# An encoder layer on one Trainium2 core: one directly multiplied half in the up projection instead of three, and whole h put together by DMA

## The chip, the cores and the metric

The kernel runs on one core of a Trainium2 chip. A core has a matrix engine (PE; its weight loads are listed as PEld), a vector engine (DVE), a scalar engine (ACT), a general engine (POOL) and a queue engine (SP). Each engine works through its own instructions strictly in order, and waits at the head of its queue until the semaphores of an instruction allow it to start. DMAs are issued from SP's queue and from POOL's queue, and all of them are carried out by the same 16 DMA engines. The metric is device microseconds of one execution, and lower is better.

## The reference

One layer over 512 tokens of width 2048, in float32. The part that matters here is the second half of it:

```
x = x + rms_norm(concat(a, p) @ w_o, post_mix_g)
h = rms_norm(x, pre_ffn_g)
up = causal_dwconv(h @ w_up, conv_w, conv_b)          # 2048 -> 2 * 5632, then 3 taps along the tokens
y = (gelu(up[:, :5632]) * up[:, 5632:]) @ w_down      # 5632 -> 2048
x = x + rms_norm(y, post_ffn_g)
```

`a` and `p` are the outputs of an attention and of a pooling branch; they are not touched by the change. The scale of the second norm, one number per token, is not applied to h itself: the kernel multiplies with x times gain and scales the rows of `h @ w_up` afterwards, with a tile `R` that holds the token scales along the free axis.

## The kernel before

**Number format.** A float32 operand is held as a high part `hi` (rounded by ACT, line 140) and a low part `lo` (the rest, a DVE subtraction, line 141). `split` makes both. `mm3` multiplies with three matmuls per block: hi by hi, hi by lo, lo by hi.

**The up projection.** The 11264 columns of `w_up` are cut into 22 units, each with a gate half and a value half of 256 columns (a half is two blocks of 128 channels, `j = 0, 1`). So there are 44 halves, each with 2048 rows of weights and 512 tokens. A half can be done in two ways.

- Directly, as `mm3` over 16 blocks of 128 rows and two `j`: 96 matmuls with 512 columns. This is done for the first `PLAIN = 3` halves: gate and value of unit 0 (`ups`), and the gate of unit 1 (`up(1, 0)`).
- As a Strassen-Winograd scheme of seven products (`seven`, `mm2`). The two weight blocks per half (`m`), the two halves of the 2048 rows (`kh`) and the two halves of the tokens make 2 x 2 blocks on each side. Each of the seven products costs 8 wide matmuls (512 columns, line 170) and 8 narrow ones (256 columns, line 176) per weight part: 56 wide and 56 narrow per half. This is done for the other 41 halves, `k = 0 .. 40`.

The seven products are numbered. Products 1, 2, 7 and 4 take a quarter of h as it is; 5, 3 and 6 take sums of quarters, held in `hs[5]`, `hs[3]`, `hs[6]`; product 7 takes a difference that is written over a quarter of h itself (`h_difference`). A quarter is a half of the rows (`k`) and a half of the tokens (`t`), and each of them lies in two tiles (`i = 0, 1`), four blocks of 128 rows to a tile.

**The sums of h.** `h_sums(i)` is called for `i = 0` and then `i = 1`. It first needs whole quarters, `whole(k, t)`: the quarter's `hi` plus its `lo`, made by a DVE addition (line 1298) into a tile from the ring `x` of the pool `p3`. That ring (`raw_x`) has four buffers of 128 x 1024 floats; the raw weights of the products 1 of most halves come from it too. Out of four whole quarters come, on DVE, `a22 - a21` (split into `hs[5]`), `a11 - a21` (kept in `differences` until `h_difference` splits it), `-(a22 - a21) - a11` (split into `hs[6]`), and one more (split into `hs[3]`). So `hs[5]` is ready first, `hs[3]` last, and one buffer of the ring per `i` is held until `h_difference`.

**The weights of the seven products.** The class `Factors` holds the list `order` of all (half, product) pairs. `load` fetches raw weight blocks on SP's queue into `raw4` (five buffers) or `raw_x` tiles; `add` adds another block from DRAM onto a raw tile by an accumulating DMA on POOL's queue, which is how the weight sums of the scheme are formed; `make` splits a raw tile into a pair of `w4` tiles (eight buffers, so four pairs). `get` asks for the next pair and prefetches `AHEAD` further ones. The first products in `order` are (0, 1), (0, 2), (0, 5), (1, 1), (0, 3).

**What sets the order.** PE's instructions run in the order in which the code calls them (`manual_schedule`). For ACT, DVE, POOL and SP a planner puts instructions into each queue, by the time at which it thinks they become ready and by their place in the code; `issue_after` puts an instruction behind a named one. A tile of a ring with no free buffer waits for a release.

**Around the change.** The output projection before it ends with `keep_x` and `turn_back`: the second half of the tokens (`t0 = 2`) is finished, transposed back by PE and split into the h tiles `hT`, while `gate_part` multiplies the first direct half piece by piece, for the first half of the tokens and then for the second. The loop over `q` ends with `gate_part(3, 2)`. `keep_x(2, ...)` squares x on ACT (line 910), a reduction (line 1054) and `rstd` (DVE line 217, then a power on POOL, line 218) make the token scales `rt`. `spread2` brings `rt` into `R`: four transposes on PE (line 223) and two DVE copies (lines 1264 and 1265). `gate` and `product` then apply the taps, gelu and the product for a unit, and store it. In the kernel before, the order of PE after `gate_part(3, 2)` is: the value half of unit 0; the first quarter of `up(1, 0)`; the transposes of `spread2`; the rest of `up(1, 0)`; and then the seven products of half 0 on.

**Keeping a product.** The products accumulate in PSUM banks `a`, `g` and `d`; `keep(k, i)` takes them out. After product 1 ACT copies bank `a` (512 columns, line 1412) into `za`; after product 2 DVE adds bank `d` to it (512 columns, line 1415); `keep_all` adds the two halves of `za` (256 columns, line 1434).

Of the kernel before, what the change touches and what calls it, by code (L numbers as in the profile page):

```python
# [15 lines left out]
P = 128  # L16
# [14 lines left out]
PLAIN = 3  # L31
# [14 lines left out]
def f32(ap):  # L46
    return ap.bitcast(F32)
# [34 lines left out]
def encoder_layer(ctx: ExitStack, tc: tile.TileContext, x, xT, vecs, rel, post_mix, post_ffn,  # L82
# [800 lines left out]
    with tc.tile_pool(name="p2", bufs=1, reuse_waits="tile") as p2:  # L883
# [137 lines left out]
        ups = [[bank(f"up0_{p}_{j}") for j in range(2)] for p in range(2)]  # L1021
# [14 lines left out]
        for q in range(5):  # L1036
            if q < 4:
                x2(2, (y21, y22)[q // 2], q // 2, columns(q % 2))
                for i in range(2):
                    turn_back(2, 2 * q + i, bank(f"xt{q}{i}"))  # L1040
            if not q:
                gate_part(3, 0, slice(2, 4))
            if q:
                gate_part(q - 1, 2)
                more_sums(1)
                weights.prefetch(q)
        keep_x(2, turn_back.last)
# [154 lines left out]
    with tc.tile_pool(name="p3", bufs=2, reuse_waits="tile") as p3:  # L1202
# [43 lines left out]
        def up(u, p, between=()):  # L1246
            ps = [bank(f"up{u}_{p}_{j}") for j in range(2)]
            between = list(between)
            for i in range(4):
                w = weights.get(f"w{p}{u}_{i}")  # L1250
                factors.prefetch(4 - len(weights.specs) + weights.used)
                for kb in range(4 * i, 4 * i + 4):
                    for j in range(2):
                        mm3(ps[j], part(w, j, slice(kb % 4 * P, (kb % 4 + 1) * P)), g_both(hT, kb),
                            kb == 0, kb == KD - 1)
                step = between.pop(0) if between else None
                if step:
                    step()
            return ps

# [33 lines left out]
        def h_sums(i):  # L1294
            def whole(k, t):
                v = raw_x(f"q{k}{t}").rearrange("p (a b) -> p a b", a=4)
                hi, lo = quarter(k, t, i)
                nc.vector.tensor_add(v, f32(hi), f32(lo))
# [23 lines left out]
        class Factors:  # L1322

            RAW, AHEAD = 10, 4

            def __init__(self):
                n = 2 * NU - PLAIN

                self.alone = 0, n - 1
                place_of = {1: 0, 6: 8, 2: 2, 7: 10, 5: 4, 4: 12, 3: 6}
                begin = [(0, 1), (0, 2), (0, 5), (1, 1), (0, 3)]
                end = [(n - 1, 5), (n - 2, 6), (n - 1, 3), (n - 1, 1), (n - 2, 7), (n - 1, 6), (n - 2, 4),
                       (n - 1, 7), (n - 1, 2), (n - 1, 4)]
                order = sorted((7 * k + at, k, i) for k in range(n) for i, at in place_of.items())
                self.order = begin + [(k, i) for _, k, i in order if (k, i) not in begin + end] + end
                self.raw, self.made, self.loaded, self.used = {}, [], 0, 0

            def block(self, k, m, kh):  # L1340
                return w_up[(PLAIN + k) // 2, (PLAIN + k) % 2, m, kh]

            def load(self, k, i):
                def raw(what, tile_, m, kh):
                    nc.sync.dma_start(tile_, self.block(k, m, kh))
                    self.raw[k, what] = tile_

                if i == 1 and (k, "w") not in self.raw:
                    raw("w" if k in self.alone else "x", raw4("wx") if k == self.alone[0] else raw_x("wx"), 0, 0)
                elif i == 5 and k == self.alone[0]:  # L1350
                    raw("x", raw4("wx"), 0, 0)
                    self.add(k, "x", 1, 0)
                elif i == 5 and k == self.alone[1]:
                    raw("w", raw_x("wx"), 0, 0)
                    raw("x", raw_x("wx"), 1, 0)
                elif i == 3:
                    raw("y", raw4("wy"), 1, 1)
                elif i == 2:
                    raw("z", raw4("wz"), 0, 1)

            def add(self, k, what, m, kh):
                nc.gpsimd.dma_start(self.raw[k, what], self.block(k, m, kh), accum_op=ALU.add)  # L1362

            def make(self, k, i):
                what = {1: "w" if k in self.alone else "x", 3: "y", 7: "y", 2: "z"}.get(i, "x")
                v = self.raw[k, what]
                if (k, i) == (self.alone[1], 5):
                    nc.vector.tensor_add(v, v, self.raw[k, "w"])
                hi, lo = w4("wfh"), w4("wfl")
                split(hi, lo, v)  # L1370
                if len(self.made) == 2:
                    self.third = split.last, split.rest
                if i == 1 and k not in self.alone:
                    self.add(k, "x", 1, 0)
                elif i == 5:
                    self.add(k, "x", 1, 1)
                elif i == 6:
# [367 lines left out]
```

## Time and profile before

| | |
|---|---|
| median of 3 runs | 1860.05 us (1859.49 to 1861.0) |
| the profiled execution: time | 1858.89 us |
| its span, first to last instruction | 1857.1 us |
| DVE busy over the span | 83% |
| ACT busy over the span | 58% |
| POOL busy over the span | 16% |
| bytes moved by DMA | 426.01 MB |

The span is what the profile's times are counted from; the time of the execution is 1.79 us longer than it. Start times in the timelines below are microseconds from the start of the span. A matmul's duration in a timeline covers its way through the array, and successive matmuls overlap; so the price of a matmul is read from the distance between starts, not from its duration.

### The profile page before, as it was taken

Reading aid. Unit: us, or ns where it says so; the run is one execution under the profiler, and the core shown is the slowest. Engines: PE = TensorE matmul, PEld = TensorE weight load, DVE = VectorE, ACT = ScalarE, POOL = GpSimd, SP = SyncE. Lnnn points to the kernel's source line nnn. Section 1 sums busy time; section 2 is a strip of 40 time slices with the busy share of each in tenths; the row PEclk is TensorE's granted clock in tenths of the full one; section 3 lists DMA queues with packets and bytes.
Section 4 is the critical chain, followed back from the end, with each engine's and each line's share of the span. In section 5 each row is a group of like instructions: output and inputs, shape, how many; then the busy total and the mean of one; then the engine's idle time right before and its main releaser. Section 6 shows DMA issues by size and latency. Waiting matters only on the chain.

```text
span 1857.1 us, 25452 instructions
## 1 busy us (share of the span) xinstructions
PE 1842.6 (99%) x9598; PEld 1584.3 (85%) x9598; DVE 1532.2 (83%) x1799; ACT 1084.4 (58%) x1376; POOL 302.8 (16%) x402
## 2 busy tenths in 40 slices
PE   9999999999999999999999999999999999999998
PEld 7888888888879888888888888888888888888886
DVE  6988778878588988888887888888887899899876
ACT  7654455456564666566565665666655655565553
POOL 3411001100000112212122122121121001111101
PEclk9999999999999999999999999999999999999999
DMA  8599977998987798888888988889888977777785
GB/s 319 171 319 302 322 230 233 267 264 310 326 308 202 185 220 195 205 204 200 201 200 203 207 202 195 204 206 205 199 179 288 363 224 171 193 211 178 176 230 157
DMA packets 139338, 426.01 MB, mean 229 GB/s; under 512 B 11920, under 2 KB 15376, under 8 KB 133520
## 3 DMA queue, kind: packets, MB, share of 16 engines
q0 software_dynamic: 54864, 173.56, 45.8%
q1 hardware_dynamic: 84352, 250.84, 38.8%
q8 instruction: 75, 1.23, 0.3%
q14 instruction: 47, 0.39, 0.1%
HBM read 370.35 MB, written 104.33 MB: 256 GB/s over the span
## 4 chain that ended last, share of the span: by engine, by line
PE 69%; DMA 1%; DVE 1%; issue 0%; ACT 0%; DVEq 0%; POOLq 0%; ACTq 0%
PE qa L170 16%; PE qa L176 8%; PE qg L170 8%; PE qg L176 4%; PE qd L170 4%; PE pa L162 4%; PE pa L165 4%; PE pa L164 4%; PE qd L176 2%; PE pg L162 2%; PE pg L165 2%; PE pg L164 2%; PE up L165 1%; PE up L162 1%; PE up L164 1%; PE pd L164 1%
## 5 line engine op out<-in xcount | busy, mean ns | idle before, releaser
L140 ACT ACTIVATE wfh<-wx 128x1024 fp32r<-128x1024 f32 x192 | 203.4, 1059 | 154.3 <-PE qg L170 54.4
L170 PE MATMUL qa<-gT,wfh 128*128 128x512 f32 x1152 | 288.6, 392 | 0.0
L141 DVE TENSOR_TENSOR wfl<-wx,wfh 128x1024 fp32r<-128x1024 f32 x192 | 234.6, 1222 | 61.0 <-ACT wfh L140 44.0
L170 PEld LDWEIGHTS qa<-gT,wfh 128*128 128x128 f32 x1152 | 207.2, 189 | 37.1
L1362 POOL DMA_DIRECT2D wx<-in_w_up x122 | 104.6, 858 | 502.6 <-DVE wfl L141 467.9
L140 ACT ACTIVATE wfh<-wy 128x1024 fp32r<-128x1024 f32 x96 | 101.7, 1060 | 108.5 <-PE qg L170 57.2
L170 PE MATMUL qg<-h,wfh 128*128 128x512 f32 x656 | 162.2, 389 | 0.1
L176 PE MATMUL qa<-gT,wfl 128*128 128x256 f32 x1152 | 161.4, 283 | 0.6 <-ACT zm L1422 0.6
L176 PEld LDWEIGHTS qa<-gT,wfl 128*128 128x128 f32 x1152 | 151.5, 191 | 4.9 <-ACT zm L1422 0.8
L170 PEld LDWEIGHTS qg<-h,wfh 128*128 128x128 f32 x656 | 122.9, 188 | 25.9 <-ACT zb L1418 0.5
L141 DVE TENSOR_TENSOR bl<-b,bh 128x2048 fp32r<-128x2048 f32 x56 | 127.2, 2285 | 19.1 <-ACT bh L140 11.7
L140 ACT ACTIVATE bh<-b 128x2048 fp32r<-128x2048 f32 x56 | 106.0, 1911 | 52.8 <-DVE b L1126 21.8
L141 DVE TENSOR_TENSOR wfl<-wy,wfh 128x1024 fp32r<-128x1024 f32 x96 | 117.1, 1220 | 12.6 <-ACT wfh L140 7.8
L162 PE MATMUL pa<-bh,ah 128*128 128x512 f32 x320 | 124.5, 389 | 0.0
L164 PE MATMUL pa<-bl,ah 128*128 128x512 f32 x320 | 124.5, 389 | 0.0
L165 PE MATMUL pa<-bh,al 128*128 128x512 f32 x320 | 124.5, 389 | 0.0
L141 DVE TENSOR_TENSOR wfl<-wz,wfh 128x1024 fp32r<-128x1024 f32 x48 | 58.7, 1223 | 54.2 <-PE qa L170 54.2
L176 PEld LDWEIGHTS qg<-h,wfl 128*128 128x128 f32 x656 | 89.5, 190 | 6.4
L170 PE MATMUL qd<-gT,wfh 128*128 128x512 f32 x384 | 94.9, 389 | 0.0
L176 PE MATMUL qg<-h,wfl 128*128 128x256 f32 x656 | 91.5, 282 | 0.0
L170 PEld LDWEIGHTS qd<-gT,wfh 128*128 128x128 f32 x384 | 71.9, 188 | 14.9
L170 PE MATMUL qa<-h,wfh 128*128 128x512 f32 x328 | 82.1, 392 | 0.0
(554 smaller groups left out, 4352.5 us busy)
## 6 DMA issues: line engine op xcount, KB each, us to landing
wx<-in_w_up POOLq DMA_DIRECT2D x122, 512.0 KB, 6.2
b<-in_w_down SPq DMA_DIRECT2D x32, 1024.0 KB, 7.0
wt<-in_w_o POOLq DMA_DIRECT2D x24, 1024.0 KB, 16.8
wx<-in_w_up SPq DMA_DIRECT2D x43, 512.0 KB, 5.5
wz<-in_w_up SPq DMA_DIRECT2D x41, 512.0 KB, 5.7
wy<-in_w_up SPq DMA_DIRECT2D x41, 512.0 KB, 4.7
wy<-in_w_up POOLq DMA_DIRECT2D x41, 512.0 KB, 6.7
sum<-part POOLq DMA_DIRECT2D x38, 512.0 KB, 6.4
```

What stands on the lines that cost most here:

```text
L140: rounded = nc.scalar.activation(hi, src, AF.Copy)
L141: rest = nc.vector.tensor_sub(lo, src, f32(hi))
L162: nc.tensor.matmul(ps, l[0], r[0], start=first, stop=False, skip_group_check=onto)
L164: nc.tensor.matmul(low, l[0], r[1], start=False, stop=False, skip_group_check=onto)
L165: nc.tensor.matmul(ps, l[1], r[0], start=False, stop=last, skip_group_check=onto)
L170: nc.tensor.matmul(ps, w[0][:, kb], pairs[kb][0], start=fresh and not kb, stop=last, skip_group_check=not fresh)
L176: nc.tensor.matmul(ps[:, sl], w[1][:, kb], pair[:, sl], start=False, stop=last, skip_group_check=not fresh)
L1362: nc.gpsimd.dma_start(self.raw[k, what], self.block(k, m, kh), accum_op=ALU.add)
```

## The change

`PLAIN` becomes 1: only the gate half of unit 0 is multiplied directly. The value half of unit 0 and the gate half of unit 1 become halves `k = 0` and `k = 1` of the seven-product scheme, which now has 43 halves. `Factors` moves up, in front of the loop that multiplies the direct half, and that loop prefetches the products' weights, six raw blocks at most, until `open` is set. The list begins with products 1 and 2 of the halves 0, 1 and 2, and these three halves keep the raw tiles of product 1 apart from those of product 5 (`alone`). The token scales are spread and the first gate is computed ahead of the loop over products. `whole` no longer adds on DVE: SP copies `hi` into the tile by a DMA within the core's memory, and POOL's queue adds `lo` by an accumulating DMA. `za` shrinks to 256 columns with three buffers, so product 1 and product 2 are folded when they are taken out.

```diff
-PLAIN = 3
+PLAIN = 1
...
-        ups = [[bank(f"up0_{p}_{j}") for j in range(2)] for p in range(2)]
+        class Factors:
...
+                self.alone, self.open = (0, 1, 2, n - 1), False
+                place_of = {1: 0, 6: 8, 2: 2, 7: 10, 5: 4, 4: 12, 3: 6}
+                begin = [(0, 1), (0, 2), (1, 1), (1, 2), (2, 1), (2, 2), (0, 5), (0, 3)]
...
+                if i == 1 and (k, "w") not in self.raw:
+                    raw("w" if k in self.alone else "x", raw4("wx") if k in self.alone[:3] else raw_x("wx"), 0, 0)
+                elif i == 5 and k in self.alone[:3]:
+                    raw("x", raw_x("wx") if k else raw4("wx"), 0, 0)
+                    self.add(k, "x", 1, 0)
...
+            def prefetch(self, n):
+                ahead = self.used + n + self.RAW - self.AHEAD if self.open else 6
+                while self.loaded < min(len(self.order), ahead) and n > 0:
+                    self.load(*self.order[self.loaded])
+                    self.loaded += 1
+                while len(self.made) < min(len(self.order), self.used + n):
+                    self.make(*self.order[len(self.made)])
...
+        ups = [[bank(f"up0_{j}") for j in range(2)]]
...
                 gate_part(q - 1, 2)
                 more_sums(1)
-                weights.prefetch(q)
+                factors.prefetch(q)
         keep_x(2, turn_back.last)
-        for q in range(4):
-            w = weights.get(f"w10_{q}")
-            for kb in range(4 * q, 4 * q + 4):
-                for j in range(2):
-                    mm3(ups[1][j], part(w, j, slice(kb % 4 * P, (kb % 4 + 1) * P)), g_both(hT, kb),
-                        kb == 0, kb == KD - 1)
         nc.vector.reduce_sum(total, ssq2, axis=AX.X)
         rstd(rt, total)
...
             def whole(k, t):
                 v = raw_x(f"q{k}{t}").rearrange("p (a b) -> p a b", a=4)
                 hi, lo = quarter(k, t, i)
-                nc.vector.tensor_add(v, f32(hi), f32(lo))
+                nc.sync.dma_start(v, f32(hi))
+                nc.gpsimd.dma_start(v, f32(lo), accum_op=ALU.add)
                 return v
...
+        factors.open = True
...
             if i == 1:
-                zs[k, "1"] = pair_tile("za", 1, 2)
-                nc.scalar.activation(wide(zs[k, "1"]), banks[k, "a"], AF.Copy)
+                v = zs[k, "1"] = p3.tile([P, T], F32, tag="za", bufs=3, name="za")
+                nc.scalar.activation(v, banks[k, "a"][:, :T], AF.Copy)
+                nc.vector.tensor_add(v, banks[k, "a"][:, T:], v)
             elif i == 2:
-                v = wide(zs[k, "1"])
-                nc.vector.tensor_add(v, banks.pop((k, "d")), v)
+                v, d = zs[k, "1"], banks.pop((k, "d"))
+                nc.vector.tensor_add(v, d[:, :T], v)
+                nc.vector.tensor_add(v, d[:, T:], v)
...
-            nc.vector.tensor_add(z[:, 0, :T], one[:, 0, 0], one[:, 0, 1])
+            nc.scalar.activation(z[:, 0, :T], one, AF.Copy)
...
         for i in range(2):
             h_sums(i)
-        z = up(1, 0, [spread2, lambda: product(0, gate(0, normed(ups[0])), normed(ups[1]))])
-        z = normed(z)
+        spread2()
+        gates[0] = gate(0, normed(ups[0]))
...
-            if (k, i) == (0, 6):
-                with tc.issue_after(keep.six):
-                    gates[1] = gate(1, z)
```

The rest of `Factors` moves word for word. `up` and the part of `Weights` that fetched the blocks of two halves go away. `h_difference` is still called behind the first product.

More of the change, by code (lines that the diff above doesn't have):

```diff
@@ L1022, in encoder_layer @@
+        factors = Factors()
+        ups = [[bank(f"up0_{j}") for j in range(2)]]
         gate_w = []
@@ L1244, in normed @@
             return z
[L1246 to L1259, printed above, removed]
         def spread2():
@@ L1397, in encoder_layer @@
-        factors = Factors()
+        factors.open = True
         banks, gates = {}, {}
```

109 lines of the change are left out of this document (47 added, 62 removed).

## The prediction

> **What bounds the kernel now.** I read the page first, then the waits of PE, then PE's timeline around the change.
>
> ```profile
> PE 1842.6 (99%) x9598; PEld 1584.3 (85%) x9598; DVE 1532.2 (83%) x1799; ACT 1084.4 (58%) x1376; POOL 302.8 (16%) x402
> ...
> PEclk9999999999999999999999999999999999999999
> ...
> PE m L164 <- DVE wo_1l L141: 2.7, 1, 2.7
> PE idle L133 <- DVE mhalf L129: 1.1, 1, 1.1
> ```
>
> PE is busy 99% of the span, and its longest wait anywhere is 2.7 us. So every matmul slot less is time gained, and every wait that the change puts on PE is time lost, one for one. The next rows give the price of both ways to do a half.
>
> ```profile
> 578.61 0.40 PE L162 MATMUL up<-gT,w_0h 128*128 128x512 f32 x1
> 605.84 0.60 PE L223 MATMUL R<-ident,rt 128*128 128x128 f32 x4
> 606.19 0.48 PE L162 MATMUL up<-gT,w_1h 128*128 128x512 f32 x1
> 622.62 1.98 PE L170 MATMUL qa<-gT,wfh 128*128 128x512 f32 x8
> ...
> 694.25 1.91 PE qa L176 x16
> 696.16 1.84 PE qa L170 x8
> 713.74 1.91 PE qa L176 x16
> ```
>
> At 578.61 the first full-width matmul of the value half of unit 0 starts (the last `gate_part` has just ended), and at 622.62 the first of the seven products. Between them lie two direct halves and the four transposes of `spread2` (606.19 - 605.84 = 0.35 us): 44.01 - 0.35 = 43.66 us, 21.83 us a half. In the chain of waits the same place of the scheme returns after 713.74 - 694.25 = 19.49 us: that is a half in seven products, 2.78 us a product. Eight wide matmuls of it take 1.84 us, 0.23 us each.
>
> **The gain.** Two halves change their way: 2 x (21.83 - 19.49) = 4.68 us less on PE. This is all that can be gained; the list of the last products, the down projection and everything ahead of 578.61 keep their PE work. 0.2% of the time, 3.7 us, is about what a measurement of this kernel can tell from no change.
>
> **What the direct halves covered, first the token scales.** Two direct halves stood between the last piece of h and the first product that needs a sum of h. They were 44 us of PE work that needs only h itself. Now PE meets the transposes of `spread2` directly behind `gate_part(3, 2)`, because they are called ahead of the loop over products and PE keeps the order of the calls.
>
> ```profile
> 575.33 0.88 DVE L144 SCALAR_TENSOR_TENSOR gT<-xt,vec,gT 128x256 fp32r<-128x256 f32 x2 [0.15 <-ACT gT L143]
> 575.58 1.05 ACT L910 ACTIVATE junk<-x 128x1024 f32<-128x1024 f32 x1
> ...
> 576.62 1.05 ACT L140 ACTIVATE w_2h<-w_2r 128x1024 fp32r<-128x1024 f32 x1
> ...
> 579.80 1.04 ACT L140 ACTIVATE w_3h<-w_3r 128x1024 fp32r<-128x1024 f32 x1
> 580.75 1.04 ACT L910 ACTIVATE junk<-x 128x1024 f32<-128x1024 f32 x1
> 582.02 0.15 DVE L1054 TENSOR_REDUCE small<-small 128x4 f32<-128x8 f32 x1
> 582.21 0.17 DVE L217 TENSOR_SCALAR rt<-small 128x4 f32<-128x4 f32 x1
> 582.53 1.87 POOL L218 TENSOR_TENSOR rt<-rt,mhalf 128x4 f32<-128x4 f32 x1 [21.88 <-DVE rt L217]
> ```
>
> The last piece of h is split until 576.21. The squares (first and last of four are shown) stand behind it on ACT, with two weight roundings among them, and `rt` is there at 582.53 + 1.87 = 584.40. The changed loop prefetches the same number of weight pairs at the same places, so ACT's queue looks alike. The transposes want to start at 578.6 and can at 584.5: 5.9 us of standing PE, with all products behind it. Even with no rounding among the squares (two times about 1.0 us) it is about 4 us. So the first wait alone takes back what the two halves gain.
>
> **Second, the sums of h.** Behind the transposes come the six products 1 and 2, 6 x 2.78 = 16.7 us, then (0, 5), which reads `hs[5]`. PE gets to it at 584.85 + 16.7 = 601.55, and to the first block of `i = 1` (its fifth wide matmul) at 602.5. When is `hs[5]` whole? In the kernel before the additions of DVE start directly behind the token scales:
>
> ```profile
> 582.28 1.22 DVE L1298 TENSOR_TENSOR q<-gT 128x1024 f32<-128x1024 f32 x1
> 605.26 1.22 DVE L141 TENSOR_TENSOR h<-q,h 128x1024 fp32r<-128x1024 f32 x1
> 614.27 1.22 DVE L141 TENSOR_TENSOR h<-q,h 128x1024 fp32r<-128x1024 f32 x1
> ...
> wx<-in_w_up POOLq DMA_DIRECT2D x8, 512.0 KB, 7.0
> wx<-in_w_up SPq DMA_DIRECT2D x6, 512.0 KB, 4.0
> q0 software_dynamic: 2456, 7.23, 39.4%
> ...
> wx<-in_w_up POOLq DMA_DIRECT2D x122, 512.0 KB, 6.2
> t<-in_w_down POOLq DMA_DIRECT2D x12, 1024.0 KB, 15.9
> zqk<-z SPq DMA_DIRECT2D x8, 512.0 KB, 9.1
> rw02h<-rwh SPq DMA_DIRECT2D x2, 512.0 KB, 3.0
> ```
>
> There `hs[5]` is whole at 606.5 and `hs[3]` at 615.5, under cover of the direct halves. The change takes eight additions off DVE, 8 x 1.22 = 9.8 us, and puts 8 copies of 512 KB on SP's queue and 8 accumulating DMAs of 512 KB on POOL's. The trace shows no DMA from SBUF to SBUF. The nearest rows are those of the window from 560 to 660: a plain 512 KB load lands after 4.0 us, an accumulating one after 7.0 us. Bounds from the rows of the whole run: 3.0 us (`rw02h`, a copy out of SBUF) and 9.1 us (`zqk`) for the first leg; 6.2 us (the same add, whole run) and 15.9 us (1 MB, within DRAM) for the second. Below nothing they can't be, since each DMA must land before the next step reads it. I take 4.0 and 7.0, which are of this size, place and queue. In that window the accumulating queue moved 7.23 MB in 39.4 us of all 16 engines, so adds follow each other at 0.524 MB / 7.23 MB x 39.4 = 2.9 us.
>
> The steps on ACT and DVE have these rows:
>
> ```profile
> L140 ACT ACTIVATE wfh<-wx 128x1024 fp32r<-128x1024 f32 x192 | 203.4, 1059 | 154.3 <-PE qg L170 54.4
> ...
> L141 DVE TENSOR_TENSOR wfl<-wx,wfh 128x1024 fp32r<-128x1024 f32 x192 | 234.6, 1222 | 61.0 <-ACT wfh L140 44.0
> ```
>
> Now the chain, with 1.1 us for an ACT and 1.2 us for a DVE step. The copies of `i = 0` land while the scales are made. Their adds stand behind the power on POOL's queue, which is called first: they start at 584.4 and land at 591.4, 594.3, 597.2, 600.1. From them: difference 595.5, `hs[5]` of `i = 0` 597.8, the second difference 599.0, the sum of product 6 at 600.2. Only now a buffer of the ring `x` is free, for it has four and `i = 0` fills them; the next ones follow at 602.6 (split of product 6's sum) and 603.8 (of product 3's). So the second round is a whole DMA chain later: first quarter of `i = 1` at 600.2 + 4.0 + 7.0 = 611.2, second at 602.6 + 11.5 (a place behind in the adds) = 614.1, difference 615.3, split 617.6. PE stands from 602.5 to 617.6: **15.1 us**.
>
> (0, 5) then needs 1.87 us more, and (0, 3) reaches its fifth wide matmul 0.92 us later, at 620.4. It needs `hs[3]`, so the fourth quarter of `i = 1`. If the planner splits the first kept difference (`h_difference`) early, that quarter gets its buffer and lands at about 620, and `hs[3]` is whole at 622.9: **2.5 us**.
>
> **The sum.** 5.9 + 15.1 + 2.5 - 4.7 = +18.8 us on the 1858.9 us of the profiled execution: 1877.7 us. That execution lies 1.2 us under the median of 1860.05, so 1878 stands for either.
>
> **Edits priced at nothing.** These are `keep` and `keep_all`; their cover is the slack in the steady part:
>
> ```profile
> L1415 DVE TENSOR_TENSOR za<-qd,za 128x512 f32<-128x512 f32 x41 | 28.1, 685 | 9.9 <-PE qd L176 9.9
> ...
> L1412 ACT ACTIVATE za<-qa 128x512 f32<-128x512 f32 x41 | 23.8, 581 | 0.0
> ...
> 674.76:1338.52 663.76, 663.18 (x3810) 585.51 (x3810) 550.03 (x647) 404.33 (x493) 142.76 (x170) 1.00 0.88 202
> L1437 DVE TENSOR_TENSOR z<-qa,z 128x256 f32<-128x256 f32 x41 | 17.1, 416 | 0.3 <-ACT z L1436 0.3
> L1434 DVE TENSOR_TENSOR z<-za 128x256 f32<-128x256 f32 x41 | 17.0, 415 | 0.0
> L1436 ACT ACTIVATE z<-qa 128x256 f32<-128x256 f32 x41 | 15.8, 385 | 30.6 <-PE qa L170 30.5
> ```
>
> Per half DVE trades 685 + 415 ns for three 256-column additions like line 1437, +0.15 us; ACT trades 581 ns for two copies like line 1436, +0.19 us. The window row's columns are PE, PEld, DVE, ACT, POOL: in 34 halves DVE was idle 113.7 us, 3.3 us a half. Were that gone, 43 x 0.15 = 6.5 us would show. The early loads of weights take buffers that the dropped blocks of direct halves had. The raw tile of (1, 5) comes from the ring `x`, so it queues on SP behind the h tiles; loaded at about 615 it is split at 628.5 by the legs above, where PE wants it at about 628 (four products after 617): 0 to 4 us, taken as 0.
>
> **Two places where the Trainium skill differs.** PE never stood longer than 2.7 us in this trace, and the granted clock is 9 tenths or more in every slice. The Trainium skill, "TensorE: Matmul & The Clock Gate", Part 1, says that an idle window of about 3.4 us halves PE's clock until about as long a busy stretch has passed. No run here shows it yet. By that rule a matmul burst behind the last long wait loses some 1.7 us, an estimate by that page, and the sum would be 1879 instead of 1878; behind the first wait the loss is swallowed by the second.
>
> The trace's 7.0 us for an accumulating 512 KB stands against the Trainium skill, "DMA: Bandwidth & Descriptors", section "Anatomy of one DMA — SWDGE (gpsimd) path": about 2.0 us plus the bytes at 436 GB/s, so 3.2 us. The trace doesn't agree; by the page both rounds of adds would land about 3.8 us earlier, and the sum would be some 7.6 us less, 1870.
>
> **Rivals.**
> - *Third round.* The first kept difference holds its buffer until late, as in the kernel before. Then the last quarter waits for the buffer that the sum of product 6 frees, at 619.4, lands 11.0 us later, and `hs[3]` is whole at 633.9: 13.5 us in place of 2.5, **1888.7 us**. For it: `h_difference` is called only behind the first product. Against it: all that it waits for in queue and data is there by then.
> - *Short chain.* The adds leave before the power, since h is whole at 576.2 and the copies need not wait for it: first add lands 8.2 us earlier; legs of 3.0 and 6.2 us save 1.8 us more in the second round. Waits 5.9, 5.1 and 2.5: **1867.7 us**. Against it: the additions on DVE stood behind the scales in the kernel before though DVE had idle time.
> - *Hidden sums.* `hs[5]` by 602.5, so 15 us earlier than my chain. Then only the token scales cost: 1858.9 + 5.9 - 4.7 = **1860.1 us**, no difference.
> - *Faster.* One mechanism: PE reaches the transposes when `rt` is already there and `hs[5]` is whole behind the six products; place 578.6 and 602.5 (then 595.9 instead), price none, **1854.2 us**. It decides from waits under 1.0 us in all. Against it: the squares can't start ahead of 575.6, and the power alone takes 1.87 us.
> - *Worse.* The ring `x` also holds up SP's queue: a copy that waits for a buffer stands ahead of weight loads, and (1, 5) and (2, 5) come late, 4 us each on top of the third round: **about 1897 us**. Both legs at their far ends (25 us a round in place of 11) would end there too, or beyond.
>
> **How the numbers follow.** Forecast 0.42, third round 0.22, short chain 0.19, hidden sums 0.09, worse 0.05, faster 0.03. The first three hold 0.83 of the chance and reach from 1867.7 to 1888.7; widened by 4 us below for shorter legs and by 7 us above for longer ones: 1864 to 1896. Faster by over 0.2%: 0.03; within: 0.09; slower: 0.88.
>
> **What would show it.** Right: PE waiting at line 223 for the power, some 5.9 us; then PE waiting at a wide matmul of product (0, 5) for DVE's split of `hs[5]`, with the release going back to a POOL add; a smaller wait in (0, 3); a steady part with 19.49 us a half. Wrong: no wait at line 223, or `hs[5]` whole before 602, or waits for weights instead of h, or a steady part that is slower.

## The result, and the profile after

| | before | after |
|---|---|---|
| median | 1860.19 us (1859.49 to 1861.0) | 1907.82 us (1904.92 to 1908.66, 4 runs) |
| the profiled execution | 1858.89 us | 1907.87 us |
| its span | 1857.1 us | 1906.0 us |
| mean granted clock of PE | 0.999 | 0.985 |

The changed kernel is slower: 1.0253 times the time before, with an interval of 1.0237 to 1.0268. That is 47.6 us; the two profiled spans differ by 48.9 us. The sign was forecast; the time lies 12 us above the range's upper end, 1896.

First the page of the changed kernel, its line of engine shares and the row of the granted clock in 40 slices:

```profile
PE 1852.9 (97%) x9630; PEld 1592.5 (84%) x9630; DVE 1542.6 (81%) x1850; ACT 1102.8 (58%) x1435; POOL 319.5 (17%) x418
PEclk9999999999998699999999999999999999999999
```

PE is busy 97% where it was 99%, and the clock falls in slices 13 and 14, from 572 to 667 us (a slice is 47.65 us): the end of the direct half and the first products. Next the waits of PE in the changed kernel; behind the colon stand the total in us, how often, and the longest:

```profile
PE qg L170 <- DVE h L141: 23.1, 2, 22.4
PE qa L176 <- ACT zm L1407: 7.0, 3, 5.6
PE R L223 <- POOL rt L218: 4.8, 1, 4.8
PE m L164 <- DVE wo_1l L141: 2.8, 1, 2.8
PE qg L170 <- ACT zb L1403: 2.7, 1, 2.7
```

The wait for `wo_1l` was there before. The others are new, and PE's timeline of the changed kernel shows their places (start, duration, and in brackets the idle time ahead of it):

```profile
585.97 1.11 PE L223 MATMUL R<-ident,rt 128*128 128x128 f32 x4 [4.78 <-POOL rt L218]
606.88 1.20 PE L170 MATMUL qg<-h,wfh 128*128 128x512 f32 x4 [0.72 <-DVE h L141]
630.47 2.08 PE L170 MATMUL qg<-h,wfh 128*128 128x512 f32 x4 [22.38 <-DVE h L141]
636.92 4.18 PE L170 MATMUL qg<-h,wfh 128*128 128x512 f32 x8 [2.67 <-ACT zb L1403]
651.46 2.08 PE L176 MATMUL qa<-gT,wfl 128*128 128x256 f32 x8 [5.61 <-ACT zm L1407]
668.84 1.21 PE L176 MATMUL qa<-gT,wfl 128*128 128x256 f32 x8 [0.69 <-ACT zm L1407]
```

In order: the transposes of the token scales, the first and the second half of product (0, 5), which read `hs[5]`, then (0, 3), (0, 7) and a product of the next half. The waits come to 4.78 + 0.72 + 22.38 + 2.67 + 5.61 + 0.69 = 36.85 us. From 669 on the steady part is what it was. This row of the windows of the changed kernel is the one of before moved by 48.9 us (columns: stretch, length, then PE, PEld, DVE, ACT, POOL busy, then PE's clock, DMA share, GB/s):

```profile
723.66:1387.42 663.76, 663.76 (x3814) 586.23 (x3814) 553.86 (x682) 410.08 (x528) 142.81 (x170) 1.00 0.88 203
```

PE is full at full clock. The chain of waits of the changed kernel goes through the place where PE stood (start, duration, what):

```profile
584.92 5.76 DMA q<-gT
...
591.25 0.85 POOL q L1356
...
593.93 10.45 DMA q<-gT
...
606.83 1.15 DVE q L1369
...
608.03 3.15 DMA q<-gT
...
615.25 12.71 DMA q<-gT
...
628.05 1.23 DVE q L1367
...
631.61 6.54 DMA wx<-in_w_up
...
638.71 9.18 DMA wx<-in_w_up
```

Two rounds of copy and add run one behind the other, as the ring of four buffers forces them to: the second round's copy starts at 608.03, when DVE has read a tile of the first. Behind them comes a weight load that starts only at 631.61, behind the h tiles. The transfers of the window 584 to 632 of the changed kernel (queues: packets, MB, share of 16 engines; issues: count, size, median us to landing):

```profile
q0 software_dynamic: 4591, 5.57, 71.6%
q1 hardware_dynamic: 4784, 6.23, 36.2%
...
q<-gT SPq DMA_DIRECT2D x8, 512.0 KB, 6.0
q<-gT POOLq DMA_DIRECT2D x8, 512.0 KB, 9.8
```

The shares of the two queues add up to 71.6 + 36.2 = 108% of the 16 engines over 48 us, so packets of the two overlap in time. The adds take 9.8 us in the median, where 7.0 was taken.

DVE's rows of the second round show what stood ahead of the last part of `hs[5]`:

```profile
625.38 1.23 DVE L1364 TENSOR_TENSOR q<-q,q 128x1024 f32<-128x1024 f32 x1 [1.75 <-DMA q<-gT]
628.05 1.23 DVE L1367 TENSOR_TENSOR q<-q,q 128x1024 f32<-128x1024 f32 x1 [1.45 <-DMA q<-gT]
629.20 1.22 DVE L141 TENSOR_TENSOR h<-q,h 128x1024 fp32r<-128x1024 f32 x1
```

The difference for `hs[5]` is formed at 625.38, when the second quarter has landed. Its low part (629.20) then stands in DVE's queue behind the other difference (628.05), which needs the third quarter; the add of 12.71 us in the chain is that quarter's.

Last, the same stretch as a whole, from 580 us to the point 1157.1 us before the end of the span, in the kernel before:

```profile
580.00:700.00 120.00, 120.00 (x634) 103.55 (x633) 108.08 (x122) 69.19 (x82) 20.57 (x23) 1.00 0.74 186
```

and in the changed kernel:

```profile
580.00:748.90 168.90, 131.35 (x695) 113.59 (x695) 117.90 (x141) 84.72 (x109) 37.53 (x40) 0.86 0.92 208
```

DMA work grew from 120 x 0.74 = 89 us of all 16 engines to 168.9 x 0.92 = 155 us. Into the old 120 us that would be a share of 1.3; over no stretch of ten us between 580 and 650 was it above 1.20. DVE has 118 us to do where it had 108, though eight additions left it.

**Where the 48.9 us are.** Waits 36.85; less the gain of 4.7; 2.6 by which the direct half ends later (its transposes are wanted at 585.97 - 4.78 = 581.2, before at 578.6); some 3 us behind the products, where a matmul waits 1.9 us for a transfer (0.6 before) and the granted clock is 0.94 from 1470 to 1500 (1.00 before); and about 10 us in which PE was busy at a lower clock (busy time times missing clock, summed over windows of ten us; its 131.35 us of work would be about 121 at full clock). Together 48.

### The profile page after: what moved, and what is told of

Same layout as the page of the kernel before. It is cut to its first block, busy times and chain, and to the rows that moved or that the text cites. A ratio compares the mean times of both kernels' runs of the same rounds, so it can differ in the third digit from the quotient of the medians.

```text
span 1906.0 us, 25711 instructions
## 1 busy us (share of the span) xinstructions
PE 1852.9 (97%) x9630; PEld 1592.5 (84%) x9630; DVE 1542.6 (81%) x1850; ACT 1102.8 (58%) x1435; POOL 319.5 (17%) x418
## 4 chain that ended last, share of the span: by engine, by line
PE 66%; DMA 4%; DVE 1%; ACT 1%; issue 0%; POOL 0%; POOLq 0%; DVEq 0%; ACTq 0%; SPq 0%
PE qa L170 16%; PE qa L176 8%; PE qg L170 8%; PE qg L176 4%; PE pa L164 4%; PE pa L162 4%; PE qd L170 4%; PE pa L165 4%; PE pg L164 2%; PE pg L162 2%; PE pg L165 2%; PE qd L176 2%; DMA q<-gT 2%; DMA wx<-in_w_up 1%; PE pd L164 1%; PE pd L165 1%
## 5 line engine op out<-in xcount | busy, mean ns | idle before, releaser
L140 ACT ACTIVATE wfh<-wx 128x1024 fp32r<-128x1024 f32 x200 | 211.8, 1059 | 180.3 <-PE qg L170 58.5
L141 DVE TENSOR_TENSOR wfl<-wx,wfh 128x1024 fp32r<-128x1024 f32 x200 | 244.4, 1222 | 78.5 <-ACT wfh L140 63.7
L170 PE MATMUL qa<-gT,wfh 128*128 128x512 f32 x1200 | 304.0, 396 | 0.0
L170 PEld LDWEIGHTS qa<-gT,wfh 128*128 128x128 f32 x1200 | 218.0, 191 | 39.2
L1061 POOL DMA_DIRECT2D wx<-in_w_up x128 | 110.9, 867 | 529.0 <-DVE wfl L141 473.2
L170 PE MATMUL qg<-h,wfh 128*128 128x512 f32 x688 | 173.7, 394 | 25.8 <-DVE h L141 23.1
L176 PE MATMUL qa<-gT,wfl 128*128 128x256 f32 x1200 | 169.8, 285 | 7.0 <-ACT zm L1407 7.0
L170 PEld LDWEIGHTS qg<-h,wfh 128*128 128x128 f32 x688 | 130.4, 190 | 54.6 <-DVE h L141 24.5
L176 PEld LDWEIGHTS qa<-gT,wfl 128*128 128x128 f32 x1200 | 159.5, 193 | 12.3 <-ACT zm L1407 8.0
L140 ACT ACTIVATE bh<-b 128x2048 fp32r<-128x2048 f32 x56 | 106.0, 1912 | 52.6 <-DVE b L1198 21.8
L176 PEld LDWEIGHTS qg<-h,wfl 128*128 128x128 f32 x688 | 95.6, 194 | 6.9
```

The lines of the kernel that those rows point to most:

```text
L140: rounded = nc.scalar.activation(hi, src, AF.Copy)
L141: rest = nc.vector.tensor_sub(lo, src, f32(hi))
L170: nc.tensor.matmul(ps, w[0][:, kb], pairs[kb][0], start=fresh and not kb, stop=last, skip_group_check=not fresh)
L176: nc.tensor.matmul(ps[:, sl], w[1][:, kb], pair[:, sl], start=False, stop=last, skip_group_check=not fresh)
```

## The experiments

Each run stood beside runs of the kernel before on the same chip, whose medians lay between 1860.7 and 1864.0 us; ratios are to that median. The letters of the theories are explained in the texts that were written before each run.

### The form of the sums, with one direct half

**The sums on DVE again, the rest as changed.**

```diff
-                nc.sync.dma_start(v, f32(hi))
-                nc.gpsimd.dma_start(v, f32(lo), accum_op=ALU.add)
+                nc.vector.tensor_add(v, f32(hi), f32(lo))
```

> The changed kernel with one part undone: whole h is added by DVE again, no DMA within the core. Theory A (the sums of h by two rounds of DMAs are what PE waits for): DVE has all it needs at about 584.8, hs[5] is whole some 20 us earlier than 630.4, so the 22.4 us wait falls under 10 us and the time comes to about 1885 us (1875 to 1892). Rival B (weights that come late, on DMA queues that are full anyway, set the time): the wait moves to a weight and the time stays above 1900.

1899.93 us, 1.0214 (1.0197 to 1.0231). Taking the DMAs back returns 8 of 47.6 us; A's number is off by 15. B's 1900 is met within the spread (the runs lie from 1898.1 to 1901.5), and the waits did move to weights as B says, but not for B's reason: the DMA queues weren't full. The waits of PE in that run:

```profile
PE qa L176 <- DVE wfl L141: 18.7, 2, 14.5
PE qa L176 <- ACT zm L1406: 5.9, 3, 4.5
PE R L223 <- POOL rt L218: 5.7, 1, 5.7
```

No wait for h is left: PE now waits for low parts of weights, which DVE makes in the same queue. Its transfers between 584 and 632, in 40 slices of 1.2 us:

```profile
GB/s 270 215 389 58 0 0 0 0 0 0 0 0 0 0 0 0 0 0 0 0 0 0 0 75 355 85 355 75 184 263 317 229 287 276 335 307 246 280 283 253
```

For 19 slices, 23 us, nothing at all is loaded. SP's next load waits 27.2 us, until 611.1, for a tile that DVE's step at line 1371, one of the sums of h, frees.

**Copy by DMA, the low part added by DVE** (line 1356 becomes `nc.vector.tensor_add(v, v, f32(lo))`).

> The changed kernel with the accumulating leg alone undone: SP still copies the high parts, DVE adds the low parts on top. Theory A1 (a round lasts 22 us because an add of 512 KB in rows of 1 KB keeps all 16 DMA engines busy for 3.3 us): the copies alone land within 8 us, the split of hs[5] is ready at least 10 us earlier than 630.4, and the time lies between that of DVE sums (1900) and the changed kernel: about 1898. Rival (the copies, or the four buffers of the ring, are what a round waits for): within 3 us of 1907.8.

1902.51 us, 1.022 (1.0205 to 1.0235). The accumulating leg is worth 5 us here, so the time lies between the two others, though 4 us above A1's number. The waits spread over weights and h; the longest are 6.4 us for a weight part and 5.1 us for h.

**The sums on POOL's engine** (the two DMAs become one `nc.gpsimd.tensor_add(v, f32(hi), f32(lo))`).

> The changed kernel with whole h added by POOL's own engine, neither by DMA nor by DVE. A 512-column addition took POOL 1.85 us in the kernel before, so one of 1024 columns some 3.7 us, a round 15 us, with DVE and the DMA engines free for weights. Theory A (what PE waits for is the sums, limited by whatever makes them): hs[5] is whole at about 611 where it was 630, and the time is 1880 to 1890, under both other ways (1908 by DMA, 1900 by DVE). Rival (the list and the missing cover set the time, whoever adds): 1898 or more.

1911.07 us, 1.0268 (1.0246 to 1.0291): the rival's number. A POOL add takes 2650 ns on average, and DVE's steps stretch beside it; DVE's timeline of that run:

```profile
590.81 3.40 DVE L1363 TENSOR_TENSOR q<-q,q 128x1024 f32<-128x1024 f32 x1 [2.79 <-POOL q L1355]
...
596.69 1.21 DVE L1366 TENSOR_TENSOR q<-q,q 128x1024 f32<-128x1024 f32 x1
```

The same operation takes 3.40 us while POOL adds (586.11 to 596.49) and 1.21 us behind it. DVE is not relieved: from 584 to 634 us it is busy 44.05 us, where in the run with the sums on DVE it was busy 40.73. So this run doesn't show that the time is the same whoever adds; POOL's adds made DVE slower.

### Token scales, buffers and the clock

**The token scales behind the six products 1 and 2.**

```diff
-        spread2()
-        gates[0] = gate(0, normed(ups[0]))
...
+            if (k, i) == (2, 2):
+                spread2()
+                gates[0] = gate(0, normed(ups[0]))
```

> The changed kernel with the transposes of the token scales and the first gate moved behind the six products. Theory A: the 4.8 us wait and the slow clock behind it disappear, but PE only comes earlier to product (0, 5) and waits there longer, so the time stays within 3 us of 1907.8. Rival C (each wait costs its own length): about 8 us less, 1900.

1907.39 us, 1.0251 (1.0236 to 1.0267), no change. The wait at the transposes is gone, and the waits for `h` grow from 23.1 to 34.6 us. So the 4.8 us there cost nothing as long as `hs[5]` is late: PE only gets sooner to the place where it stands.

**Raw weights of (1, 5) and (2, 5) out of the ring `x`.**

```diff
-                    raw("x", raw_x("wx") if k else raw4("wx"), 0, 0)
+                    raw("x", raw4("wx"), 0, 0)
```

> The changed kernel with the raw weights of (1, 5) and (2, 5) in the ring raw4 and not in the ring x, which the tiles of h fill until 631. Theory A': the late wait of 5.6 us ahead of product (0, 7) goes back to these weights, so it goes and 3 to 8 us with it: about 1902. Rival E: it goes back to the full DMA engines, and nothing changes (within 2 us).

1906.55 us, 1.025 (1.0235 to 1.0266). The wait of (0, 7) falls from 5.6 to 0.7 us, as the mechanism says, but the wait for `hs[5]` grows from 22.4 to 25.0 us and 1.5 us for a weight part comes in: nothing is won. That is E's number, though the late tile was the reason for the wait.

**Matmuls in the waits that keep PE's clock up** (8 ahead of the transposes, 44 in the middle of (0, 5), 17 more ahead of the products (0, 5), (0, 3) and (0, 7); nothing reads their result).

> The changed kernel with extra matmuls on a tile of zeros, into a bank that nobody reads, where PE stands: ahead of the transposes, in the middle of product (0, 5), ahead of (0, 3) and (0, 7). They leave out nothing and fill waiting time, so that PE's clock isn't halved behind the waits. Theory G (the slow clock adds to the waits): the granted clock stays near 1.00, and since the next wait swallows what (0, 1), (0, 5) and (0, 3) lost, some 2 to 4 us are won: about 1904. Rival (slow clock and waits add up): 10 us won, 1897. If the clock costs nothing here, or the extra matmuls overshoot: 1908 or more.

1906.2 us, 1.0234 (1.0216 to 1.0252). The mean clock rises from 0.985 to 0.993 (from 580 to 650 us: from 0.71 to 0.87), so only about half of the loss was brought back. The time falls by 1.6 us, and the two intervals overlap, so that can't be told from nothing. That a faster product only gets sooner to the next wait fits this, but isn't shown apart.

### One part alone, in the kernel before

**The new list of products and the folded `za`** (`begin` and `alone` as changed, `keep` and `keep_all` as changed; three direct halves, sums on DVE).

> The kernel before with the new list (products 1 and 2 of three halves first) and the folded za alone; three direct halves, DVE sums. Theory A: no wait comes of it, within 3 us of the kernel before. Rival F: 43 halves with more work on DVE and ACT, 6 us or more slower.

1867.78 us, 1.0041 (1.0025 to 1.0056): 6 us slower. They are lost mostly at one place, where (0, 3) waits 4.1 us for ACT's copy `zb` and the granted clock is 0.83 from 640 to 660. That is F's number, but not its mechanism: from 690 to 1350 us PE is busy throughout, at a clock of 1.00.

**The sums by DMA** (line 1298 becomes the two DMAs).

> The kernel before with one part of the change alone: whole h by a copy and an accumulating DMA. Theory A: the two rounds of some 22 us start at about 583 and end at about 628, where PE gets to product (0, 5) at 628.2, so at most a few us show: 1860 to 1866. Rival D (the DMAs cost by themselves, by the load on the DMA engines, whatever covers them): over 1875.

1890.37 us, 1.0161 (1.0146 to 1.0176): 30 us, rival D's number, though two direct halves cover the sums. The waits of PE in that run:

```profile
PE qa L170 <- ACT wfh L140: 5.3, 1, 5.3
PE qa L176 <- ACT zm L1423: 4.2, 1, 4.2
...
PE qd L170 <- ACT wfh L140: 2.9, 1, 2.9
PE qg L170 <- ACT wfh L140: 2.9, 1, 2.9
...
PE qd L176 <- DVE wfl L141: 1.9, 1, 1.9
```

PE never waits for h. It waits for parts of weights: ACT and DVE work in order, the splits of weights stand behind steps on h, and these stand for the DMAs. ACT's timeline ahead of the wait of 2.9 us that ends at 629.56 shows one such place:

```profile
627.50 1.06 ACT L140 ACTIVATE h<-q 128x1024 fp32r<-128x1024 f32 x1 [13.78 <-DVE q L1307]
628.47 1.04 ACT L140 ACTIVATE wfh<-wz 128x1024 fp32r<-128x1024 f32 x1
```

Theory A had looked at h alone.

**Only the copy by DMA, there too.**

> The kernel before with the copying leg alone: SP copies the high parts, DVE adds the low parts. Three direct halves cover it. Theory A1 (the accumulating leg is what makes a round 22 us long): a round is some 10 us of DMA and DVE, both end before 620, PE needs them at 629: 1860 to 1865. Rival (any DMA in the ring of four buffers does it): over 1872.

1866.14 us, 1.0029 (1.0015 to 1.0042). With DVE adding the low part in place of the accumulating leg, 24 of the 30 us are gone.

**The sums by DMA, called behind the last direct half.**

```diff
+        z = up(1, 0, [spread2, lambda: product(0, gate(0, normed(ups[0])), normed(ups[1]))])
         for i in range(2):
             h_sums(i)
-        z = up(1, 0, [spread2, lambda: product(0, gate(0, normed(ups[0])), normed(ups[1]))])
```

> The kernel before with whole h by DMAs (as in e3_dma_in_before, 1890), but with the sums called behind the last direct half, so that its weights and its scales come first in the queues of ACT and DVE. Theory H (in e3 PE waits for weights whose rounding stands on ACT or DVE behind a step of h that waits for its DMA): the waits ahead of the products 1 and 2 go, the DMAs start as early as before, and the time falls by 5 to 15 us, to 1875 to 1885. Rival (the DMAs themselves are late): within 3 us of 1890.

1897.1 us, 1.0187 (1.0165 to 1.0209): worse by 7. The waits for weights are gone, as theory H says, but not the time: called later, the sums come later, and PE waits for `h` itself, 13.99 and 14.35 us.

### One, two and three direct halves

Two direct halves: `PLAIN = 2`, `up(1, 0)`'s loop stands again behind the first, the token scales are spread in the middle of it. With the sums on DVE:

> The changed kernel with two direct halves in place of one (the value half of unit 0 is direct again and stands ahead of the six products), DVE sums, and the token scales spread in the middle of that half. One direct half is 21.8 us of cover. Theory A (what is lost is lost because the cover of two direct halves is gone, 44 us for some 33 us of DVE work on h): most of the waits go, hs[5] is whole at about 612 where PE wants it at 618; the best case is 2.3 us under the kernel before, 1858; with DVE full, some waits of a few us remain: 1856 to 1870. Rival F (the new order and the folding cost by themselves, all along the steady part): over 1875.

1884.67 us, 1.0119 (1.0101 to 1.0137): F's number, but not its mechanism. From 690 to 1380 us PE is busy throughout, at a clock of 1.00; what is lost is lost ahead of that, in waits for weight parts (5.4, 3.1 and 2.0 us) and for ACT's copy `zm` (5.8 us). Theory A, that the cover is what is missing, had the place right and the size wrong. With the sums on POOL's engine:

> Two direct halves as in e8_plain2_dve (1885), with the sums added by POOL. Theory A: DVE, full from 585 to 634 in e8, loses 9.8 us of work, and the 21.8 us of the second direct half cover the two rounds of POOL, so the waits of e8 shrink to a few us: 1860 to 1870, 1858 at best. Rival (POOL's longer steps hold up its own queue of weight additions): 1880 or more.

1894.2 us, 1.0173 (1.0152 to 1.0195): the rival's number again; whether POOL's own queue was the reason, or DVE's longer steps as above, wasn't separated. With the sums by DMA:

> The changed kernel with two direct halves, token scales spread in the second, sums by DMA. The same with sums on DVE took 1884.7 us. Theory L: PE asks for hs[5] 21.8 us later than in the changed kernel, at some 624, and it is whole at about 630: a wait of 6 us, no wait at the transposes, the weight wait as there or less: 1868 to 1878 us. Theory T (a direct half less costs 15 to 17 us whatever forms the sums; DMA costs 8 us over DVE): 1888 to 1896 us.

1903.82 us, 1.0234 (1.0203 to 1.0264), above both numbers. The waits of PE there:

```profile
PE qd L176 <- DVE wfl L141: 22.3, 1, 22.3
PE qa L176 <- DVE wfl L141: 6.7, 2, 6.2
```

and DVE's timeline ahead of the long one, which ends at 645.45:

```profile
642.37 1.23 DVE L1384 SCALAR_TENSOR_TENSOR q<-q,q 128x1024 f32<-128x1024 f32 x1 [3.44 <-DMA q<-gT]
643.51 0.74 DVE L1291 SCALAR_TENSOR_TENSOR cb<-z,vec,cb 128x511 f32<-128x511 f32 x1
644.17 1.22 DVE L141 TENSOR_TENSOR wfl<-wz,wfh 128x1024 fp32r<-128x1024 f32 x1
```

PE wants a weight part at 623.2. It stands on DVE behind a step that needs the last DMA of the sums (landed 642.3). PE asks for h late enough now, and still stands 22 us for the same transfers. Last, three direct halves, the new list, the folded `za`, and the sums by DMA:

> The kernel before with the new list of products and the folded za (1867.8 us) and with the sums by DMA. In the kernel before the DMAs alone added 30 us, with waits that went from weights to weights, since the first kept sum was wanted 16.7 us earlier than with the new list. Theory L: with the new list (0, 5) comes 60 us behind the last piece of h, hs[5] is whole some 46 us behind it, so no wait for h; the weights behind the h tiles in the queues have the same 16.7 us: 1868 to 1876 us. Theory T or plain addition of the two: 1890 to 1898 us.

1894.52 us, 1.0179 (1.016 to 1.0198): the sum of the two parts, not theory L. The series:

| direct halves | sums on DVE | sums by DMA | difference |
|---|---|---|---|
| 3 (with the new list) | 1867.8 | 1894.5 | 26.7 |
| 2 | 1884.7 | 1903.8 | 19.1 |
| 1 | 1899.9 | 1907.8 | 7.9 |

With the sums on DVE each direct half less costs 16.9 and 15.3 us. A direct half leaves DVE 16.9 us free (four low parts of weights at 1.22 us in 21.83 us of PE), a half in seven products 3.3, so DVE loses 13.6 us of free time with each. That is of the same order, and no more than an argument.

### The sums without their forming

**Sums from the high parts alone.** The sums leave out the low parts; no copy, no add. The differences and splits on DVE and ACT stay.

```diff
-            a22, a21 = whole(1, 1), whole(0, 1)
-            nc.vector.tensor_sub(a22, a22, a21)
+            a22 = new(1, 1)
+            nc.vector.tensor_sub(a22, high(1, 1), high(0, 1))
...
```

> The changed kernel, its sums of h formed from the high parts alone: no copies, no accumulating DMAs and no additions; the differences and splits of DVE and ACT stay (the low parts are left out of the sums). Theory L (what stands is the lateness of the DMA sums): no wait for hs[5], since it is whole some 6 us after the squares, at about 592; what is left over before is the token scales' 4.8 us, a weight wait of up to 6 us and some clock, less the gain of 4.7: 1864 to 1873 us. Theory T (the stretch behind the direct half is too short for all that DVE, ACT and the queues have to do there, however the sums are formed: differences, splits, weight pairs of the products, the first gate): the waits only move to weight parts, as they did with the sums on DVE (1899.9 us); that run less the 9.8 us of DVE additions is about 1890, so 1882 to 1895 us.

1889.14 us, 1.0143 (1.0127 to 1.0158): theory T. Its waits of PE:

```profile
PE qa L176 <- DVE wfl L141: 7.4, 2, 4.9
PE R L223 <- POOL rt L218: 5.7, 1, 5.7
PE qa L176 <- ACT zm L1407: 5.4, 3, 4.4
```

and two of its windows:

```profile
590.00:600.00 10.00, 10.00 (x52) 8.59 (x52) 9.33 (x9) 5.95 (x8) 0.00 (x0) 0.90 0.03 14
...
610.00:620.00 10.00, 8.41 (x43) 6.61 (x42) 7.65 (x13) 4.22 (x6) 1.72 (x2) 0.87 1.00 265
```

From 590 to 600 PE works through products while DVE, 93% busy, works on h: the DMA share is 0.03. DVE forms no low part of a weight between 584.84 and 605.03, and SP's next weight load waits 16.0 us for a buffer that a DVE step on h frees. From 610 on the loads run at 1.00 and PE waits for what they bring. So of the 47.6 us about 19 (1907.8 - 1889.1) go with the forming of the sums by DMA, and 27 (1889.1 - 1861.8) come without it. The 27 aren't all one thing: the wait for the token scales (5.7 us) and whatever the new list and the folded `za` cost here (6 us alone) are among them.

**The low parts of the sums by ACT, as zeros.** As the last one; the sums' low parts are left out here too, so eight steps of DVE go to ACT.

> The changed kernel with the sums of h formed from the high parts alone (as in e16_high_only, 1889.1 us), and besides the eight low parts that the splits of these sums and differences make are written by ACT as zeros instead of by DVE as a difference. That takes 8 x 1.14 = 9.1 us off DVE behind the direct half and puts some 8 us on ACT; DMAs, rings and queues stay. Theory T with DVE as the full resource (it ran there without a gap from 586 to 617, and split no weights for 20 us of it): weight pairs are made some 9 us earlier and so loaded earlier: 1877 to 1883 us. Rival, the loads themselves or the rings are what is short there (its DMA share was 0.9 to 1.0 from 610 to 640): 1886 to 1891 us, no change within 3 us. If ACT takes the place of DVE: above 1891 us.

1885.58 us, 1.0114 (1.008 to 1.0148), between the two numbers and, by the intervals, not to be told from the last run. Its windows show why it can't decide: in the ten us from 590 DVE has gaps, and ACT has none.

```profile
590.00:600.00 10.00, 10.00 (x51) 8.73 (x50) 6.82 (x9) 10.00 (x13) 0.00 (x0) 0.87 0.18 58
```

The full queue moved from DVE to ACT, which needs as many steps for a weight pair as DVE. Which of the queues or rings is the shortest in the 27 us stays open. More buffers in ring `x` weren't tried, nor this run with the token scales spread later. No version was faster than the kernel before.

## Why the prediction was right and wrong

**Right: the sign and the places; the gain fits.** The balance above closes with the gain of 4.7 us, though no run measured it alone. The steady part stayed full, and `keep` and `keep_all` cost nothing in it. PE stands first at the transposes, then at the fifth wide matmul of (0, 5), released by a DVE split that goes back to a POOL add; all three were named.

**The token scales, 5.9 us:** 4.8 in the trace. As a cost it is less: moved away, the time didn't change, because the next wait swallowed it. The prediction added waits that lie in one chain. This is its first error of method.

**`hs[5]`, 15.1 us: 23.1, and it is the step that was worked out most closely.** The ring's two rounds came as forecast. Three sizes and an order were off. The copies of `i = 0`, priced as hidden under the squares, started at 584.92 behind a weight load that held SP's queue; so the first add started at 591.25, not 584.4. The adds were to land 2.9 us after one another from 591.4 on; the third landed at 604.4. And in the second round the second quarter was there at 625.4, not 614.1; the third quarter's add took 12.7 us, where 7.0 had been taken (the bound from the whole run reached to 15.9). That quarter isn't part of `hs[5]`, but the split of `hs[5]` stood behind it on DVE; the prediction had the split ahead. In the kernel before it stood behind as well: line 1309 at 604.11, the split shown in the prediction at 605.26. The legs were read from a window in which the engines had room. With eight copies and eight adds in 48 us the queues' shares add to 108%.

**`hs[3]`, 2.5 us:** 2.67, and right by chance: the row names ACT's `zb`, not h. `h_difference` did run early, so the third round stayed away, as forecast.

**Weights of (1, 5), priced at 0: 5.6 us.** The raw tile was loaded at 631.6, not 615; ACT's copy `zm` stood behind its rounding. Mended alone it gave nothing back: one chain again.

**The clock, left out of the sum:** about 10 us of PE's work in the trace, not the 1.7 us estimated for the last wait alone; in the time, 1.6 us for about half of it brought back, which can't be told from nothing. The Trainium skill, "TensorE: Matmul & The Clock Gate", Part 1, would have PE at half clock behind each long wait, and the trace agrees (0.50 between 610 and 640).

**The step that failed most** is one that priced nothing: "Two halves change their way: 2 x (21.83 - 19.49) = 4.68 us less on PE", with only the sums of h and the scales behind it. It took a direct half as PE work, and put the loads and splits of weights beside it at nothing ("The early loads of weights take buffers that the dropped blocks of direct halves had."). In the prediction's terms all but the sums was 5.9 - 4.7 = +1.2 us. The run with sums that cost nothing to form still lost 27 us, with no wait for h, 8.3 us of waits for weight parts and 5.4 for ACT's copy `zm`: the direct halves were also the time in which DVE, ACT and the DMAs dealt with h and filled the rings with weights. The forming itself, 15.1 + 2.5 = 17.6 us in the prediction, came to 19; that this is near is chance, as the same DMAs cost 30 us in the kernel before and 8 over DVE in the changed one.

A half in seven products needs seven weight pairs in 19.5 us in place of four in 21.8. The rows for it stood in the prediction, used for something else: DVE's 3.3 us of idle time a half, and 1.22 us a step. With the sums on DVE some 24 steps on h (8 additions, 8 sums and differences, 8 low parts) are about 28 us; two direct halves hide them, six products don't. That 27 us are lost without the sums' forming is shown, and so is that weight loads and splits stood behind the work on h. That DVE's free time is the resource that was short is argued from the series, and the run with ACT's zeros couldn't part DVE from ACT.

**The parts don't add with one direct half.** With three, the list costs 6 us, the DMAs 30, and both together 33; with one the DMAs cost only 8 more than DVE. The reading is that they hit the same queues, and whichever is late hides the rest.

The formula of the Trainium skill, "DMA: Bandwidth & Descriptors", section "Anatomy of one DMA — SWDGE (gpsimd) path" (an estimate of 3.2 us for such an add), was rightly set aside: 9.8 us median. But that page's section "Issuing engines are not separate DMA queues", by which transfers of all queues interleave on the same 16 engines, agrees with the trace (the two queues' 108%) and should have entered the sum.

## What to carry to other kernels

Before a stretch of PE work is made shorter, add up what every other engine and the DMAs do beside it, over the same stretch, and set it against the new length; a slow form of a product can be the cover in which rings fill. Waits in one chain aren't summed: take one away and see which comes next. A step moved from a busy engine to a DMA still holds that engine's queue if the next step there waits for it.

## What was not expected of the hardware

**A short wait can lower the clock, or not.** Both kernels wait some 2.7 us for `wo_1l` at about 519. The window around it in the kernel before:

```profile
500.00:540.00 40.00, 37.30 (x178) 30.63 (x177) 33.01 (x41) 22.07 (x35) 0.72 (x1) 1.00 0.88 309
```

and in the changed kernel, where the granted clock is 0.96 over the same 40 us:

```profile
500.00:540.00 40.00, 36.74 (x165) 29.42 (x164) 31.20 (x39) 19.86 (x32) 0.72 (x1) 0.96 0.87 305
```

The wait was 2.70 us there and 2.75 us here. A wait of 2.7 us at this place lowered the clock to 0.96 in the run with the token scales behind the six products, and left it at 1.00 in the run with the sums by DMA in the kernel before. What decides stays open.

**DVE and POOL's engine block one another.** A DVE step of 1.21 us took 3.40 us beside a POOL add, and POOL's adds in that run took between 2.34 and 3.39 us. The Trainium skill, "SBUF — State Buffer", section "SBUF: two separate sides", has it that a DVE operation with two inputs in SBUF and a POOL operation that reads SBUF hold a shared pair of ports by turns, each for its whole length; the trace agrees.
